# Layer 0's output projection: buffers over other memory, loads in another order, one store on another queue, one context turn later

## The chip, the cores and the metric

The kernel runs on one core of a Trainium2 chip. A core has TensorE (PE: matrix products; PEld is its weight load), VectorE (DVE), ScalarE (ACT) and GpSimd (POOL) for elementwise work, and SyncE (SP), whose queue issues most of the transfers; ScalarE has a queue for transfers too. Every engine works through its own instructions in order and waits on semaphores for the others. The metric is the time of one launch on the device in microseconds (us).

## The reference

Two layers of a diffusion transformer over 1024 latent and 256 context tokens of width 1024, in fp32. Layer 0 is multi-head latent attention (16 heads), layer 1 differential attention (8 heads). What the change touches is the end of layer 0, which for every token is

```python
o = attention(...)                       # (tokens, 1024)
o = o * silu(gate)                       # gated()
x = layer_norm(ALPHA * x + g * (o @ out_w[0]), ln_g[0], ln_b[0])
ctx = layer_norm(ALPHA * ctx + g_c * (o_c @ out_w[0]), ln_g[0], ln_b[0])
```

where `g` and `g_c` are rows of 1024 numbers (the adaptive gates of the latent and of the context tokens), and `x` and `ctx` are what layer 0 was given. The rows so normalised are modulated and become layer 1's input.

## The kernel before

The tokens are ten tiles of 128: tiles 0 to 7 are latent, 8 and 9 context. Products in fp32 are made of three matmuls on operands split into a high and a low part (`mm3`, L184 to L187). A split of an operand is a cast on ScalarE and a subtraction on VectorE (`split`, L176 and L177).

**Layer 0's attention** works head by head. A unit of it is two key tiles: scores on TensorE into a pair of PSUM banks (`pair`), the exponential on ScalarE into a buffer `p32`, a cast to half precision, the remainder on GpSimd (`softmax_parts`, L713 to L715), and later the values on TensorE (L781 to L784); `retire` and `flush` do the values of units that are still pending. The block's end (`fin`, L792 and L793) divides on VectorE into `op`, and at the last head every block stores its part of `op` into the DRAM tensor `o_d[0]` (L797, SP's queue). For the last head the order of the query blocks is 0, 2, 1: the context rows come before the latent rows 512 to 1023.

**The context tiles.** During the last block the two context tiles are loaded from `o_d[0]` with their gates from `sg_d[0]` and multiplied on VectorE (`load_ctx`, L863, L864). `turn_out` transposes a tile on TensorE by eight matmuls with the identity (L834) into two PSUM banks and splits it into the operands of the projection. Tile 8's operands lie in the two buffers `ows`, tile 9's in `rr` and one of the two buffers `cs`. Then `mm_out` makes the projection, a half of the 1024 columns at a time: 8 steps of 3 matmuls of 128x512. The four half products of the context stand in two pairs of banks, `yctx`. TensorE's order is written by hand (`manual_schedule`, MAN = 'P'): turn tile 8, the values of the one unit, turn tile 9, half product of tile 8, `flush` (the values of the last unit), three more half products.

**The output stage** (`with ow_ctx, spool("o0") as op0`) has its own pool of buffers, allocated by `ot`. Its loads are issued from SP: `load_gate` (a gate row to all partitions), `load_res` (what the layer was given), `load_o` (`o` and its gate `g`, multiplied on GpSimd at L993). For every tile `turns` transposes and splits (into `tH`, `tL`), `z_half` multiplies half a product by the gate row, adds the residual and takes statistics (L1004 to L1006), `z_norm` normalises (L1010 to L1012, with two small steps on GpSimd, L159 and L160), `z_keep` writes what layer 1's end needs, and `z_turn` transposes the normalised rows, modulates them on ScalarE and splits them into layer 1's input `h1H`, `h1L` (L1023 to L1029). TensorE's order is by hand here too: turn of tile 0, `z_turn(8)`, half product of tile 0, `z_turn(9)`, turn of tile 1, second half product, and so on.

**Memory.** A pool lays its buffers out in the order in which its tags are first asked for, and a buffer waits for the readers of whatever lay there before (`reuse_waits="tile"`). The pool `o0` lies over the end of the attention's pool. That one has, from the place where `o0` begins, and in kB per partition (1 kB = 1024 B): the end of `op` (1.9), small ones, `rsw` (4), `rr` (4), `stkH`, `stkL`, `stqH`, `stqL`, `stpH`, `stpL` (2.5 each), `ows` (2 x 4), `cs` (2 x 4), `KH0`, `KL0` (2.5 each), `p32` (3 x 4). The buffers of `o0` have 4 kB each (`res`, `o`, `z`, `tH`, `tL` twice, the others once). Before, their order is `gate01` (context gate row, later the norm's gain), `res`, `o`, `g`, `gate00` (latent gate row), `z`, small ones, `tH`, `tL`, `hb`, `gb1`. So `gate01` lies over `op` and `rsw`, the first `res` over `rsw` and `rr`, `o` and `g` over the `st` buffers, and `z` over `ows` and a `cs`.

**The order of the other engines' work**, SP's queue among them, is written by a planner, which starts from the program's order and its own forecast of times. A transfer is issued when SP comes to it and its buffer is free; what is behind it on SP waits with it. PSUM has eight banks; the stage's banks `c`, `b`, `d`, `a` take the place of the attention's three pairs and its two banks `d`.

Of the kernel before, what the change touches and what calls it, by code (L numbers as in the profile page):

```python
# [9 lines left out]
F32 = mybir.dt.float32  # L10
F32R = mybir.dt.float32r
# [6 lines left out]
P = 128  # L18
D = 1024
KT = D // P  # L20
# [8 lines left out]
H0, NOPE, ROPE, V0 = 16, 64, 32, 64  # L29
# [24 lines left out]
def hybrid_kernel(  # L54
# [7 lines left out]
    pe, act, dve, pool, sp = nc.tensor, nc.scalar, nc.vector, nc.gpsimd, nc.sync  # L62
# [6 lines left out]
    def nm(s):  # L69
        uid[0] += 1  # L70
        return f"{s}_{uid[0]}"
# [650 lines left out]
    def retire(part):  # L722

        u = pend[0]
        u[0](*u[1], part)
        if part:
            pend.pop(0)
            if u[2] is not None:
                u[2]()

    def flush():
        while pend:
            retire(0)
            retire(1)
# [20 lines left out]
    def units0(h, b):  # L755
# [30 lines left out]
        def fin():  # L786
            pv = hold["pv"]
            if h % 2 == 0 and b == 0:
                opair[0] = w0("op")
            op = opair[0]  # L790
            rc = w0("rc")
            dve.reciprocal(rc[:, :nt], pv[:, :nt, V0])  # L792
            dve.tensor_tensor(op[:, c0 // P:c0 // P + nt, (h % 2) * V0:(h % 2) * V0 + V0], pv[:, :nt, :V0],  # L793
                              rc[:, :nt].rearrange("p (t o) -> p t o", o=1).to_broadcast([P, nt, V0]), op=ALU.mult)
            if h % 2 == 1 and (b == 2 or h == H0 - 1):
                t0, t1 = (c0 // P, c0 // P + nt) if h == H0 - 1 else (0, NT)
                sp.dma_start(o_d[0].rearrange("(t p) d -> p t d", p=P)[:, t0:t1, (h // 2) * P:(h // 2 + 1) * P],  # L797
                             op[:, t0:t1, :])

        return [((lambda kc=kc: st_of(kc)), do_pv, fin if kc == kcs[-1] else None) for kc in kcs]  # L800
# [38 lines left out]
    def mm_out(y, tH, tL, c):  # L839
        for k in range(KT):  # L840
            mm3(y, tH[:, k, :], tL[:, k, :], oH[:, k, c], oL[:, k, c], k == 0, k == KT - 1)

    yctx = {}
    for h in range(H0):
# [8 lines left out]
        if last:  # L853
# [14 lines left out]
            tv = lambda x: x.bitcast(F32R).rearrange("p (a b) -> p a b", a=KT)  # L868
            tctx = {8: (tv(w0("ows")), tv(w0("ows"))), 9: (tv(w0("rr")), tv(w0("cs")))}
            with tc.manual_schedule(engines={ENG[c] for c in MAN}):  # L870
                for t in (8, 9):
                    tb = pair()
                    turn_out(octx[t][0], *tctx[t], [tb[:, :512], tb[:, 512:]])
                    if t == 8:
                        retire(0)
                        retire(1)
                for t in (8, 9):
                    yctx[t] = pair()
                    for hh in range(2):
                        c = slice(hh * 512, hh * 512 + 512)  # L880
                        mm_out(yctx[t][:, c], *tctx[t], c)
                        flush()
        else:
            kq = chain(prod_k(h + 1), prod_q(h + 1, 0))
# [88 lines left out]
        dve.tensor_tensor(vic, kci, lcf[:, 1:2], op=ALU.mult)  # L973

    with ow_ctx, spool("o0") as op0:
        ot = lambda tag, bufs=2, shape=[P, D], dt=F32: op0.tile(shape, dt, tag=tag, bufs=bufs, name=nm(tag))
        rows_of = lambda t: slice(t * P, (t + 1) * P)
        halves = [slice(hh * 512, hh * 512 + 512) for hh in range(2)]
        gate, gb, res, ol, zs, bs_, tHL = [None] * 2, [], {}, {}, {}, {}, {}
# [1 line left out]
        def load_gate(s):  # L981
            gate[s] = ot(f"gate0{s}", 1)
            bcast_row(gate[s], gates_d[0, s:s + 1, :])
# [5 lines left out]
        def load_o(t):  # L989
            ol[t], g = ot("o"), ot("g", 1)  # L990
            sp.dma_start(ol[t], o_d[0][rows_of(t), :])
            sp.dma_start(g, sg_d[0][rows_of(t), :])
            pool.tensor_tensor(ol[t], ol[t], g, op=ALU.mult)  # L993
# [37 lines left out]
        load_gate(1)  # L1031
        load_res(8)
        load_o(0)
        load_gate(0)
        load_res(9)
        load_o(1)
        for t in (8, 9):
            for hh in range(2):
                z_half(t, hh, yctx[t][:, halves[hh]])
            z_norm(t)  # L1040
# [528 lines left out]
```

## Time and profile before

| | |
|---|---|
| time, median of 3 runs | 1848.2 us (1843.51 to 1848.47) |
| the profiled execution | 1848.19 us |
| its span (first to last instruction) | 1846.4 us |
| mean granted TensorE clock | 0.972 |
| PE busy | 1693.7 us (92%) |
| DVE busy | 1240.0 us (67%) |
| ACT busy | 1104.3 us (60%) |
| POOL busy | 811.8 us (44%) |

The stage in question runs from about 790 to 970 us of the span. How the views are read: a row of the time line has the start, the duration, the engine, the line, the operation, what it writes and reads, a count, and in brackets how long the engine stood idle before it and for whom. A row of the waits has who waited for whom, the sum, how often, and the longest. A row of the table by stretches has the stretch, its length, the busy time and count of PE, PEld, DVE, ACT and POOL, the granted clock, the share of the DMA engines and the GB/s. `SPq` is SP's queue.

### The profile page before, as it was taken

The numbers are of one execution on the slowest core, as the hardware profiler recorded it, in microseconds if no ns is written. First come the engines' busy times: TensorE is split into PE (matmuls) and PEld (weight loads), VectorE is DVE, ScalarE is ACT, GpSimd is POOL, SyncE is SP. The second block draws the span as 40 slices with busy tenths as digits, with TensorE's granted clock in tenths as the row PEclk, the third lists the DMA queues.
The fourth block names the chain that finished last, engine by engine and source line by source line (L and its number), as shares of the span: only waits on it lengthen the run. The fifth ranks groups of instructions, "written<-read, shape, count | busy, mean of one in ns | idle before, by whom it ended". The sixth has DMA issues, their size and how long they took to land. (4 is left out here: it accounts for less than half of the span.)

```text
span 1846.4 us, 36569 instructions
## 1 busy us (share of the span) xinstructions
PE 1693.7 (92%) x14468; PEld 1239.2 (67%) x14468; DVE 1240.0 (67%) x2054; ACT 1104.3 (60%) x2223; POOL 811.8 (44%) x719
## 2 busy tenths in 40 slices
PE   8889999999999999888999999999999999986998
PEld 3889975666666665566776676757575767665776
DVE  6545765565565566627764878777777777879574
ACT  3433047777877778824444675767676776757442
POOL 1434026766867766827542313131313132435454
PEclk8999899999999999999999999999999999999999
DMA  8245631101111121236433212121212122223231
GB/s 290 82 117 170 195 109 35 45 21 44 40 38 32 41 56 48 73 114 211 148 126 84 76 52 73 51 73 51 68 40 58 49 55 62 64 63 109 92 130 69
DMA packets 111225, 154.84 MB, mean 84 GB/s; under 512 B 13415, under 2 KB 84679, under 8 KB 111054
## 3 DMA queue, kind: packets, MB, share of 16 engines
q1 hardware_dynamic: 103182, 145.17, 26.3%
q10 hardware_dynamic: 7872, 7.34, 1.2%
q8 instruction: 114, 1.87, 0.4%
q14 instruction: 57, 0.47, 0.1%
HBM read 98.65 MB, written 27.07 MB: 68 GB/s over the span
## 5 line engine op out<-in xcount | busy, mean ns | idle before, releaser
L715 POOL TENSOR_TENSOR pl<-p,ph 128x1024 f16<-128x1024 f32 (+1 forms) x176 | 364.6, 2077 | 148.9 <-ACT ph L714 122.6
L1251 ACT ACTIVATE p<-ps_b,mx 128x512 f32<-128x512 f32 (+1 forms) x384 | 230.3, 617 | 86.0 <-DVE mx L1247 81.9
L713 ACT ACTIVATE p<-ps_a,esc 128x1024 f32<-128x1024 f32 (+1 forms) x176 | 189.0, 1074 | 96.1 <-PE ps_a L771 89.7
L695 DVE TENSOR_REDUCE mx<-ps_a 128x1 f32<-128x1024 f32 x128 | 155.5, 1223 | 134.8 <-PE ps_a L693 134.7
L714 ACT CAST ph<-p 128x1024 f16<-128x1024 f32 (+1 forms) x176 | 177.1, 1006 | 5.5
L1245 DVE TENSOR_REDUCE mx<-ps_b 128x1 f32<-128x512 f32 x256 | 165.9, 683 | 0.0
L784 PE MATMUL ps_d<-Vh,pl 128*128 128x65 f16 x1344 | 145.9, 194 | 4.7 <-POOL pl L715 4.6
L781 PE MATMUL ps_d<-Vh,ph 128*128 128x65 f16 x1344 | 148.1, 195 | 0.0
L783 PE MATMUL ps_d<-Vl,ph 128*128 128x64 f16 x1344 | 146.9, 193 | 0.0
L1228 PE MATMUL ps_b<-KS,QS 128*128 128x512 f16 (+1 forms) x384 | 126.8, 347 | 12.6 <-DVE pl L182 6.9
L1276 POOL TENSOR_TENSOR sm<-sm,us 128x1 f32<-128x1 f32 x64 | 17.0, 265 | 272.8 <-DVE sm L1255 269.3
L781 PEld LDWEIGHTS <-ph 128*128 128x128 f16 x1344 | 123.2, 97 | 18.3 <-issue 5.1
L783 PEld LDWEIGHTS <-ph 128*128 128x128 f16 x1344 | 123.9, 98 | 12.0
L1229 PE MATMUL ps_b<-KS,Q 128*128 128x512 f16 (+1 forms) x384 | 129.5, 346 | 0.0
L769 PE MATMUL ps_a<-qH,KH 100*128 100x512 f16 x320 | 122.5, 383 | 7.5 <-ACT p L713 3.7
L182 DVE SCALAR_TENSOR_TENSOR pl<-ps_b,lcf,ph 128x512 f16<-128x512 f32 (+1 forms) x192 | 117.3, 655 | 15.0 <-ACT ph L181 14.9
L784 PEld LDWEIGHTS <-pl 128*128 128x128 f16 x1344 | 123.1, 97 | 6.1 <-POOL pl L715 6.1
L181 ACT ACTIVATE ph<-ps_b,lcf 128x512 f16<-128x512 f32 (+1 forms) x192 | 115.0, 646 | 19.7 <-PE ps_b L1264 19.7
L1264 PE MATMUL ps_b<-idr,p 128*128 128x128 f32 x640 | 103.6, 278 | 24.5 <-ACT p L1251 16.3
L770 PE MATMUL ps_a<-qH,KL 96*128 96x512 f16 x320 | 122.3, 382 | 0.0
L771 PE MATMUL ps_a<-qL,KH 96*128 96x512 f16 x320 | 121.7, 380 | 0.0
L1274 PE MATMUL ps_b<-vh,pl 128*128 128x128 f16 x640 | 111.3, 220 | 5.3 <-DVE pl L182 5.3
(412 smaller groups left out, 5294.3 us busy)
## 6 DMA issues: line engine op xcount, KB each, us to landing
ws<-in_dw SPq DMA_DIRECT2D x28, 512.0 KB, 3.9
adw<-in_ada_w SPq DMA_DIRECT2D x24, 512.0 KB, 4.7
adaw<-in_ada_w SPq DMA_DIRECT2D x16, 512.0 KB, 5.9
g<-sg_d SPq DMA_DIRECT2D x16, 512.0 KB, 3.5
sg_d<-gg ACTq DMA_DIRECT2D x40, 128.0 KB, 3.8
o_d<-op SPq DMA_DIRECT2D x7, 640.0 KB, 3.7
xt<-in_xT SPq DMA_DIRECT2D x16, 256.0 KB, 3.2
wgs<-in_w_in SPq DMA_DIRECT2D x32, 128.0 KB, 2.2
```

Source lines behind the costliest of these rows:

```text
L695: dve.tensor_reduce(mx[:, t, 0:1], ps, axis=AX.X, op=ALU.max)
L713: act.activation(p32[:, :n], st, AF.Exp, scale=esc0)
L714: act.copy(ph[:, :n], p32[:, :n])
L715: pool.tensor_tensor(pl[:, :n], p32[:, :n], ph[:, :n], op=ALU.subtract)
L769: pe.matmul(s_, kh[:nr, ks], QH[:nr, :], start=True, stop=False)
L781: pe.matmul(pv[:, t, :], ph[:, ts], Vh[:, k, h, :], start=(k == kcs[0] and t == 0), stop=False, skip_group_check=True)
L783: pe.matmul(pv[:, t, :V0], ph[:, ts], Vl[:, k, h, :], start=False, stop=False, skip_group_check=True)
L784: pe.matmul(pv[:, t, :], pl[:, ts], Vh[:, k, h, :], start=False, stop=(k == NT - 1), skip_group_check=True)
L1228: pe.matmul(out, qs[m][:, ts], ks[m][:, c0:c0 + n], start=True, stop=False)
L1229: pe.matmul(out, q1[m][:, ts], ks[m][:, c0:c0 + n], start=False, stop=True)
L1245: dve.tensor_reduce(mx[:, 2 + 2 * m + i:3 + 2 * m + i], b, axis=AX.X, op=ALU.max, negate=True)
L1251: act.activation(p[m][:, c0:c0 + n], b, AF.Exp, bias=nb, accum_out=sm[:, 2 + 3 * m + i:3 + 3 * m + i])
```

## The change

It has four parts. (1) `ot` allocates by `rot`, and the first buffer of each tag is allocated ahead of the stage in a written order: `gb1`, `gate00`, `hb`, `o`, `g`, `z`, `tH`, `tL`, `gate01`, `res`. So `gb1` lies over `op` and `rsw`, `gate00` over `rsw` and `rr`, `hb` over `rr` and `stkH`; `o` and `g` lie where they lay; `z` lies over `stpL` and `ows`, `tH` over `ows` and `cs`, `tL` over `cs`, `KH0`, `KL0` and a `p32`, `gate01` and `res` over `p32` and behind it. (2) The load of the latent gate row comes after `load_res(9)` and `load_o(1)`. (3) The last store of `op` (last head, block 1) is issued from ScalarE's queue. (4) The turn of tile 9 comes after the first half product of tile 8, ahead of `flush`.

```diff
             if h % 2 == 1 and (b == 2 or h == H0 - 1):
                 t0, t1 = (c0 // P, c0 // P + nt) if h == H0 - 1 else (0, NT)
-                sp.dma_start(o_d[0].rearrange("(t p) d -> p t d", p=P)[:, t0:t1, (h // 2) * P:(h // 2 + 1) * P],
+                (act if h == H0 - 1 and b == 1 else sp).dma_start(
+                    o_d[0].rearrange("(t p) d -> p t d", p=P)[:, t0:t1, (h // 2) * P:(h // 2 + 1) * P],
                              op[:, t0:t1, :])
...
-                for t in (8, 9):
+                def turn_ctx(t):
                     tb = pair()
                     turn_out(octx[t][0], *tctx[t], [tb[:, :512], tb[:, 512:]])
-                    if t == 8:
-                        retire(0)
-                        retire(1)
+
+                turn_ctx(8)
+                retire(0)
+                retire(1)
                 for t in (8, 9):
                     yctx[t] = pair()
                     for hh in range(2):
                         c = slice(hh * 512, hh * 512 + 512)
                         mm_out(yctx[t][:, c], *tctx[t], c)
+                        if t == 8 and hh == 0:
+                            turn_ctx(9)
                         flush()
...
     with ow_ctx, spool("o0") as op0:
-        ot = lambda tag, bufs=2, shape=[P, D], dt=F32: op0.tile(shape, dt, tag=tag, bufs=bufs, name=nm(tag))
+        ot = lambda tag, bufs=2, shape=[P, D], dt=F32, **kw: rot(op0, shape, dt, tag, bufs, **kw)
+        for tag, bufs in (("gb1", 1), ("gate00", 1), ("hb", 1), ("o", 2), ("g", 1), ("z", 2), ("tH", 2), ("tL", 2),
+                          ("gate01", 1), ("res", 2)):
+            ot(tag, bufs, [P, KT, P] if tag in ("hb", "tH", "tL") else [P, D], F32R if tag in ("tH", "tL") else F32,
+               first=True)
...
         load_gate(1)
         load_res(8)
         load_o(0)
-        load_gate(0)
         load_res(9)
         load_o(1)
+        load_gate(0)
```

## The prediction

> **What bounds the kernel now.** I read the page first, then the waits of the stretch around the changed code, then the time line of each engine and the SP queue there, and last a table by stretches. Durations are us from the start of the span. "Tile 8" and "tile 9" are the two context tiles, "tile 0" the first latent one.
>
> ```profile
> span 1846.4 us, 36569 instructions
> ```
>
> The profiled execution took 1848.19 us; the median of the runs is 1848.2, so a sum made against this trace stands for the median as it is. TensorE bounds the kernel as a whole, so what counts is where it stands still. In the waits of all engines from 785 to 850 two of its waits stand out, and one of POOL:
>
> ```profile
> POOL o L993 <- DVE bs L1006: 33.3, 1, 33.3
> ...
> PE ps_c L834 <- POOL o L993: 8.6, 1, 8.6
> ...
> PE ps_a L834 <- DVE cs L864: 2.4, 1, 2.4
> ```
>
> TensorE waits 8.6 us for POOL's gated product of tile 0 (L993) and 2.4 us for VectorE's gated product of tile 9 (L864). POOL did not wait for the statistics of L1006, which have nothing to do with its operands, but for the two loads of L993. Why these came late is told by the waits of the SP queue from 790 to 828, and its time line:
>
> ```profile
> SPq L797 <- DVE op L793: 17.9, 1, 17.9
> SPq L987 <- PE ps_a L186: 9.4, 1, 9.4
> SPq L897 <- DMA o_d<-op: 5.8, 1, 5.8
> ```
>
> ```profile
> 810.99 0.37 SPq L797 DMA_DIRECT2D o_d<-op  x1
> 817.25 0.32 SPq L897 DMA_DIRECT2D gate<-gates_d  x1
> 827.01 0.33 SPq L987 DMA_DIRECT2D res<-in_ctxr  x1
> 827.39 0.42 SPq L991 DMA_DIRECT2D o<-o_d  x1
> 827.91 0.38 SPq L992 DMA_DIRECT2D g<-sg_d  x1
> ...
> 829.30 0.49 SPq L991 DMA_DIRECT2D o<-o_d  x1
> ```
>
> SP works in order. It stood 17.9 us at the last store of the attention output, 5.8 until that store had landed (the context gate row's buffer lies over `op`), and 9.4 until TensorE had read `rr` for the last time (the buffer of `res` lies over `rsw` and `rr`). `o` and `g` of tile 0, whose own memory was long free, were behind. The price on TensorE, by stretches (length, busy time and count of each engine, granted clock, DMA share, GB/s), and its time line with one row of each step:
>
> ```profile
> 798.90:801.30 2.40, 0.02 (x1) 0.00 (x0) 2.40 (x2) 0.30 (x1) 1.21 (x1) 0.98 0.00 0
> 801.30:804.70 3.40, 3.37 (x12) 3.08 (x13) 1.18 (x2) 0.63 (x2) 0.00 (x0) 0.51 0.00 0
> 804.70:827.20 22.50, 22.46 (x117) 17.76 (x115) 2.59 (x5) 0.54 (x1) 0.00 (x0) 1.00 0.33 106
> 827.20:835.80 8.60, 0.03 (x1) 0.03 (x1) 3.89 (x7) 0.00 (x0) 2.34 (x1) 0.77 0.91 320
> 835.80:839.00 3.20, 3.20 (x17) 3.00 (x17) 2.27 (x4) 1.47 (x3) 0.75 (x2) 0.54 0.95 301
> ```
>
> ```profile
> 796.18 1.06 PE L834 MATMUL ps_a<-idr,rsw 128*128 128x128 f32 x8 [0.65 <-DVE rsw L864]
> ...
> 798.73 0.20 PE L784 MATMUL ps_d<-Vh,pl 128*128 128x65 f16 x1
> 801.33 1.94 PE L834 MATMUL ps_a<-idr,cs 128*128 128x128 f32 x8 [2.41 <-DVE cs L864]
> 802.93 0.78 PE L185 MATMUL ps_a<-oH,ows 128*128 128x512 f32 x1
> ...
> 809.38 0.21 PE L781 MATMUL ps_d<-Vh,ph 128*128 128x65 f16 x1
> ...
> 810.12 0.48 PE L185 MATMUL ps_a<-oH,ows 128*128 128x512 f32 x1
> ...
> 826.77 0.40 PE L187 MATMUL ps_a<-oH,cs 128*128 128x512 f32 x1
> 835.77 1.97 PE L834 MATMUL ps_c<-idr,o 128*128 128x128 f32 x8 [8.61 <-POOL o L993]
> ...
> 838.96 0.47 PE L185 MATMUL ps_a<-oH,tH 128*128 128x512 f32 x1
> ...
> 845.61 1.06 PE L1023 MATMUL ps_d<-idr,z 128*128 128x128 f32 x8 [0.80 <-DVE z L1012]
> ```
>
> Behind both standstills the granted clock is about half for some 3.3 us (0.51 and 0.54), and eight transposes take 1.94 and 1.97 us there against 1.06 at full clock. Three half products (24 matmuls each) run from 810.12 to 827.0, 5.64 us each; the values of the last unit take 0.74 (809.38 to 810.12). The rest of the case is what the other engines do:
>
> ```profile
> 795.06 5.04 POOL L715 TENSOR_TENSOR pl<-p,ph 128x1024 f16<-128x1024 f32 x2 [0.44 <-ACT ph L714]
> ```
> ```profile
> 797.89 0.69 DVE L177 TENSOR_TENSOR ows<-ps_a,ows 128x512 fp32r<-128x512 f32 x1 [1.86 <-ACT ows L176]
> 798.50 2.69 DVE L864 TENSOR_TENSOR cs<-cs,cs 128x1024 f32<-128x1024 f32 x1
> 801.11 0.68 DVE L177 TENSOR_TENSOR ows<-ps_a,ows 128x512 fp32r<-128x512 f32 x1
> ```
> ```profile
> 833.38 2.34 POOL L993 TENSOR_TENSOR o<-o,g 128x1024 f32<-128x1024 f32 x1 [33.27 <-DVE bs L1006]
> ...
> 836.93 0.58 ACT L176 CAST tH<-ps_c 128x512 fp32r<-128x512 f32 x1 [31.69 <-PE ps_c L834]
> ...
> 837.54 0.69 DVE L177 TENSOR_TENSOR tL<-ps_c,tH 128x512 fp32r<-128x512 f32 x1
> ```
>
> **Part 1: the turn of tile 9 half a product later.** Before, TensorE goes from the values (798.93) over the wait and the slow transposes to the first product matmul at 802.93. After, the first half product of tile 8 starts at 798.93: its first operands are split by 798.58 (797.89 + 0.69). Its later operands are ready at 801.79 (801.11 + 0.68) and wanted by the 15th matmul, at 798.93 + 14 x 0.235 = 802.22, so 0.4 us hides them. Tile 9's product is ready at 801.19, long before its transposes at 804.6. Their split needs about 3 us on ScalarE and VectorE and has the values (0.74) and a half product (5.64) over it, so it costs nothing; without that cover it would cost about 3. With no standstill I take the clock as full. The context products then end at 798.93 + 4 x 5.64 + 1.06 + 0.74, and 0.16 that the last matmul outlasts the pace: 823.45, against 827.17. **Gain 3.7.**
>
> The clock weighs here: half speed from 801.30 to 804.70 costs half of 3.4 us, 1.7. The Trainium skill, TensorE: Matmul & The Clock Gate, Part 1 (the HAM clock gate), has the clock halved after an idle window of about 3.4 us that runs freely; a standstill of 2.41 us cannot fill one. By that rule the slow stretch would have another cause and could stay: a gain of 2.0 in place of 3.7. The trace has it begin right behind the standstill, and I go by the trace.
>
> **Part 2: the buffers.** With the tags laid out in the new order, the context gate row and `res` lie over the exponentials `p32`, whose last reader is POOL's L715, done at 800.10; `o` and `g` stay where they were. So gate row, `res` and `o`, `g` of tile 0 can be issued from 800.1. Four transfers of 0.52 MB at the 320 GB/s of the stretch 827.20:835.80 take 6.6 us; first data come some 2 us behind the issue (827.39 to 833.38 is 6.0 us for three). They land by about 809, POOL's product is ready by 811.5, 12 us ahead of 823.45. Should the load of `o` have to await the landing of the last store (issued near 807, and 6 us on its way before), the product would end near 821.5: still in time. What is late next: `z` lies over `ows`, free when tile 8's product ends near 812; the gate multiplication, residual sum and norm of tile 8 take about 8 us (6.7 from 830.76 to 836.68 + 0.81 and 1.3 for the multiplication) and end near 820:
>
> ```profile
> 830.76 1.29 DVE L1005 SCALAR_TENSOR_TENSOR z<-res,z 128x512 f32<-128x512 f32 x2 [2.87 <-DMA res<-in_ctxr]
> ...
> 836.68 0.81 DVE L1012 TENSOR_SCALAR z<-z,mv 128x1024 f32<-128x1024 f32 x1 [2.72 <-POOL mv L160]
> ```
> Before, tile 9's `z` lay over an operand of the second context product; now its first half runs beside that product's second half. The two `yctx` pairs and the new banks share PSUM: tile 0's transposes go where tile 8's product lay, and need its gate multiplication done, some 10 us earlier. So nothing holds TensorE at 823.45: eight transposes of tile 0 and eight of tile 8 take 2 x 1.06; the cast and the first subtraction end 2.46 us after the transposes start (835.77 to 837.54 + 0.69), the third matmul wants them at 2.59. I take 2.2 from the end of the context products to the first matmul of tile 0; it was 11.8 (827.17 to 838.96). **Gain 9.6.**
>
> **Part 3: the order of the loads.** The latent gate row moves behind `res` and `o`, `g` of tile 9, and so on SP behind the wait of the second `g` (one buffer) for POOL's first product, which ends by 811.5. It lies over `rr`, so SP then stands until the end of the context products, and behind it stand the lambda row, the first latent `res`, both norm rows and the next loads. Gate row, lambda and `res`, 1.2 MB, land about 5.7 us after 823.45; the multiplication that wants them follows the first half product at 2.2 + 5.64 = 7.8. Hidden by 2 us; were it not, the norm of tile 0 would slip by what is missing. The lambda row stands in VectorE's order ahead of tile 9's norm, which tile 9's transposes await. It was 6.65 us from the first matmul to these (838.96 to 845.61), 0.80 of it the wait; it can be 5.64 and no wait, or with the lambda row landing late a wait of 1.5. I take 0.5. **Gain 0.5 (from -0.5 to 1.0).**
>
> **Part 4: the last store on ScalarE.** 0.37 us of issue, behind a wait until about 807 for VectorE. Behind it ScalarE has three weight loads that wait for the same values anyhow, and the casts of tile 0 at 824.6. Were it still on SP, the loads would go at 807 in place of 800 and the product would be ready near 818.5: still in time. Zero.
>
> Sum: 3.7 + 9.6 + 0.5 = 13.8, so 1848.2 - 13.8 = **1834.4 us**.
>
> What follows has its own waits (the two stretches, and a row of the waits from 845 to 970):
>
> ```profile
> 839.00:970.00 131.00, 123.42 (x600) 96.50 (x599) 94.66 (x126) 57.51 (x123) 76.06 (x52) 0.97 0.45 150
> 970.00:1840.00 870.00, 804.88 (x6432) 593.46 (x6429) 642.98 (x1234) 548.27 (x1479) 284.59 (x398) 0.98 0.24 69
> ```
> ```profile
> PE ps_d L1023 <- DVE z L1012: 6.8, 4, 3.3
> ```
>
> TensorE is idle for 7.6 of the 131 us of the tile loop. The loop's order of loads and of POOL's work shifts against TensorE, so these may change by some 4 us either way: the likeliest case's own range is 1830 to 1839.
>
> **The rivals.** (a) *The loop takes it back.* POOL is busy for 76.06 of the 131 us, and its norm steps queue behind its products; if the loop is paced by it, an earlier start ends in longer waits of the transposes for the norm. Against it: TensorE is busy for 94%, and POOL's first two products move out of the loop's start. One or two more waits like the longest, 3.3 us, take 3 to 7: about 1840. (b) *The queue is held all the same*, by a wait that I do not see, on the first load or by another order of SP that the planner writes. Then only part 1 is left: 1844.5. For it: the waits of one queue hide behind each other, as three did here. (c) *The clock by the rule of the window*: 1.7 us stay, 1836.1. (d) *Slower: the planner's order in layer 1.* Only TensorE's order is written by hand; the planner orders the others by its own forecast, which shifts. Layer 1 has 64 steps in 870 us. A worse order there that costs 0.22 us a step eats all 13.8, and 0.35 makes 1857. Against it: all of layer 1 shifts alike, and its buffers lie where they lay. (e) *The change doesn't do what it says*, no load starts earlier and the turn costs what it saves: 1848.
>
> **How the numbers follow.** Likeliest 0.70, (a) 0.10, (b) 0.06, (c) 0.05, (d) 0.05, (e) 0.04. A measurement of this kernel tells about 0.3%, 5.5 us, from no change: faster is under 1842.7. The likeliest, (a) and (c) are faster: 0.85; (b) and (e) count as the same: 0.10; slower 0.05. The range of 8 in 10 takes in (a) and the loop's spread: 1829 to 1842.
>
> **What would show it.** Right: SP issues six loads between 800 and 803; POOL's L993 runs near 810; no wait of L834 for L993; L185 of tile 8 ahead of tile 9's transposes, which take 1.06; granted clock 1.00 from 799 to 835; tile 0's first matmul near 825.6, tile 9's `z` transposes near 832. Wrong: a wait of SP in front of the six loads, a wait of L1023 over 2 us for the norm, or longer mean times from step to step in layer 1.

## The result, and the profile after

The changed kernel takes **1836.7 us** in the median (1831.31 to 1843.42), the kernel before 1844.3 us beside it: a ratio of **0.9962, interval 0.9945 to 0.9979**. A second set of runs gave 0.9969 (0.9954 to 0.9984). So 6 to 7 us are gained by these ratios (the medians differ by 7.6 and 6.7), half of the 13.8 predicted. The profiled execution of the changed kernel took 1831.31 us, its span is 1829.5 us.

One span less the other (16.9 us) says little: the first attention product (L693) stands at 273.15 and 269.16 us in two profiles of the kernel before, and at 263.87 and 269.75 in two of the changed one, long ahead of anything that was changed. So the stage is measured from an anchor close to it: the last attention product ahead of tile 8's turn that waits for GpSimd (L784). TensorE's time line of the changed kernel, one row of each step (columns as before):

```profile
779.55 0.20 PE L784 MATMUL ps_d<-Vh,pl 128*128 128x65 f16 x1 [0.83 <-POOL pl L715]
787.47 1.06 PE L835 MATMUL ps_a<-idr,rsw 128*128 128x128 f32 x8 [2.89 <-DVE rsw L865]
...
795.18 1.03 PE L835 MATMUL ps_a<-idr,cs 128*128 128x128 f32 x8
...
813.67 1.03 PE L835 MATMUL ps_c<-idr,o 128*128 128x128 f32 x8
821.59 1.94 PE L1031 MATMUL ps_d<-idr,z 128*128 128x128 f32 x8 [6.89 <-DVE z L1020]
823.18 0.78 PE L185 MATMUL ps_a<-oH,tH 128*128 128x512 f32 x1
...
830.81 1.03 PE L1031 MATMUL ps_d<-idr,z 128*128 128x128 f32 x8
...
843.78 1.09 PE L1031 MATMUL ps_d<-idr,z 128*128 128x128 f32 x8
...
942.58 1.04 PE L1031 MATMUL ps_b<-idr,z 128*128 128x128 f32 x8
```

The wait of 2.4 us at tile 9's turn and the 8.6 us at tile 0's are gone. In their place TensorE waits 6.89 us one step later, at the turn of z(8), and the eight transposes behind it take 1.94 us. By stretches (columns as before) it is the same picture: full clock to 813.7, then 7.9 us with 1.0 us of work, then half clock:

```profile
797.50:813.70 16.20, 16.20 (x71) 12.91 (x71) 2.56 (x6) 0.59 (x1) 2.40 (x1) 1.00 0.61 210
813.70:821.60 7.90, 1.01 (x10) 0.80 (x8) 6.77 (x9) 1.07 (x2) 3.06 (x3) 0.90 0.65 230
821.60:825.00 3.40, 3.30 (x11) 2.56 (x12) 3.40 (x7) 2.28 (x7) 0.28 (x2) 0.50 0.62 216
```

The loads did what they were to do. SP's queue of the changed kernel (`SPq` rows) and GpSimd's product of tile 0:

```profile
789.34 0.32 SPq L901 DMA_DIRECT2D gate<-gates_d  x1
789.70 0.43 SPq L995 DMA_DIRECT2D res<-in_ctxr  x1
790.24 0.38 SPq L999 DMA_DIRECT2D o<-o_d  x1
790.72 0.36 SPq L1000 DMA_DIRECT2D g<-sg_d  x1
...
813.63 0.32 SPq L901 DMA_DIRECT2D gate<-gates_d  x1
```
```profile
797.58 2.40 POOL L1001 TENSOR_TENSOR o<-o,g 128x1024 f32<-128x1024 f32 x1 [8.26 <-DVE cs L177]
...
817.75 0.19 POOL L159 TENSOR_SCALAR mv<-mv 128x1 f32<-128x1 f32 x1 [17.78 <-DVE mv L1018]
818.03 0.56 POOL L160 TENSOR_TENSOR mv<-mv,neghalf 128x1 f32<-128x1 f32 x1
818.56 2.34 POOL L1001 TENSOR_TENSOR o<-o,g 128x1024 f32<-128x1024 f32 x1
```

The four loads go at 789.3 to 790.7, 23 to 24 us ahead of the context products' end, and tile 0's product is done at 800. What is late stands in VectorE's time line of the changed kernel:

```profile
802.67 1.29 DVE L1012 TENSOR_TENSOR z<-ps_a,gate 128x512 f32<-128x512 f32 x2 [3.76 <-DMA ws<-in_dw]
813.87 0.69 DVE L1012 TENSOR_TENSOR z<-ps_a,gate 128x512 f32<-128x512 f32 x1 [9.91 <-PE ps_a L187]
814.47 1.28 DVE L1013 SCALAR_TENSOR_TENSOR z<-res,z 128x512 f32<-128x512 f32 x2
815.67 1.28 DVE L1014 BATCH_NORM_STATS2 bs<-z 128x6 f32<-128x512 f32 x2
816.87 0.67 DVE L1012 TENSOR_TENSOR z<-ps_a,gate 128x512 f32<-128x512 f32 x1
817.46 0.20 DVE L1018 BATCH_NORM_AGGREGATE mv<-bs 128x2 f32<-128x12 f32 x1
818.62 2.82 DVE L1020 TENSOR_SCALAR z<-z,mv 128x1024 f32<-128x1024 f32 x1 [0.96 <-POOL mv L160]
```

The two gate products of tile 8 (L1012) run at 802.67. The next instruction in VectorE's queue is not tile 8's residual (L1013) but the first gate product of **tile 9**, and that stands 9.91 us until the last matmul into tile 9's pair of banks. All of tile 8's rest, its data long there, runs behind it. In the kernel before the order is the same, at 820.73, 827.20 and 830.76 (the last row is in the prediction); there it cost nothing, since `res` landed only at 830.7. VectorE's two gate products there:

```profile
820.73 1.29 DVE L1004 TENSOR_TENSOR z<-ps_a,gate 128x512 f32<-128x512 f32 x2 [9.76 <-DMA gate<-gates_d]
827.20 0.69 DVE L1004 TENSOR_TENSOR z<-ps_a,gate 128x512 f32<-128x512 f32 x1 [5.18 <-PE ps_a L187]
```

From the turn of z(7) to the end of the span it is 887.2 and 885.6 us in two profiles before, 886.9 and 885.8 in two after (spans 1846.4, 1839.8, 1829.5, 1833.7 less the row of z(7)): layer 1 did not change.

### The profile page after: what moved, and what is told of

It is laid out like the page before. It is cut to its first block, busy times and chain, and to the rows that moved or that the text cites. A ratio compares the mean times of both kernels' runs of the same rounds, so it can differ in the third digit from the quotient of the medians.

```text
span 1829.5 us, 36574 instructions
## 1 busy us (share of the span) xinstructions
PE 1680.2 (92%) x14468; PEld 1229.2 (67%) x14468; DVE 1238.1 (68%) x2054; ACT 1104.9 (60%) x2223; POOL 812.0 (44%) x719
## 5 line engine op out<-in xcount | busy, mean ns | idle before, releaser
L784 PE MATMUL ps_d<-Vh,pl 128*128 128x65 f16 x1344 | 145.9, 194 | 3.9 <-POOL pl L715 3.9
L784 PEld LDWEIGHTS <-pl 128*128 128x128 f16 x1344 | 123.1, 97 | 5.3 <-POOL pl L715 5.3
```

The source lines that it names most:

```text
L784: pe.matmul(pv[:, t, :], pl[:, ts], Vh[:, k, h, :], start=False, stop=(k == NT - 1), skip_group_check=True)
```

## The experiments

Theory T: the order in VectorE's queue makes the 6.9 us and the half clock. Rivals: D, tile 8's data are late; L, the loop over the tiles takes back whatever comes earlier; S, the store on ScalarE's queue costs something. The table gives, for one profile of every kernel, how far behind the anchor (the L784 above) TensorE reaches a step; each number is the start of the step's row less that of the anchor's. "Context end" is the start of tile 0's transposes less the wait named in their row.

| kernel | anchor | context end | first product, tile 0 | turn z(9) | turn z(0) | turn z(7) | ratio to the kernel before |
|---|---|---|---|---|---|---|---|
| before | 790.50 | 36.7 | 48.5 | 55.1 | 68.2 | 168.7 | – |
| before_2 | 787.65 | 35.9 | 47.7 | 54.9 | 68.0 | 166.5 | – |
| changed | 779.55 | 34.1 | 43.6 | 51.3 | 64.2 | 163.0 | 0.9962 (0.9945 to 0.9979) |
| after_2 | 785.30 | 34.1 | 43.6 | 51.2 | 64.2 | 162.6 | 0.9969 (0.9954 to 0.9984) |
| u_turn | 787.56 | 35.7 | 45.2 | 52.2 | 65.2 | 164.4 | 0.999 (0.9975 to 1.0004) |
| u_bufs | 786.97 | 35.4 | 47.4 | 54.6 | 69.0 | 169.8 | 0.999 (0.9976 to 1.0005) |
| u_loads | 785.62 | 36.3 | 43.8 | 51.3 | 64.3 | 165.0 | 0.9977 (0.9965 to 0.999) |
| u_store | 787.10 | 34.1 | 43.6 | 51.2 | 64.2 | 162.6 | 0.9982 (0.9969 to 0.9995) |
| e_order | 788.24 | 34.1 | 42.6 | 49.0 | 63.7 | 161.0 | 0.995 (0.9933 to 0.9967) |
| e_pool | 782.81 | 35.3 | 42.8 | 50.4 | 65.3 | 165.4 | 0.9973 (0.9958 to 0.9989) |
| e_bank | 788.42 | 34.1 | 41.1 | 49.6 | 63.8 | 161.1 | 0.9973 (0.9962 to 0.9985) |
| e_best | 786.20 | 34.1 | 38.6 | 44.3 | 63.8 | 161.7 | 0.997 (0.9957 to 0.9983) |
| e_clear | 784.29 | 32.4 | 34.1 | 41.2 | 59.7 | 158.0 | 0.9952 (0.9934 to 0.997) |
| e_loop | 784.80 | 36.4 | 38.1 | 44.9 | 59.1 | 158.2 | 0.994 (0.9922 to 0.9959) |

**The parts undone one at a time.** First the buffers:

```diff
-        ot = lambda tag, bufs=2, shape=[P, D], dt=F32, **kw: rot(op0, shape, dt, tag, bufs, **kw)
-        for tag, bufs in (("gb1", 1), ("gate00", 1), ("hb", 1), ("o", 2), ("g", 1), ("z", 2), ("tH", 2), ("tL", 2),
-                          ("gate01", 1), ("res", 2)):
...
+        ot = lambda tag, bufs=2, shape=[P, D], dt=F32: op0.tile(shape, dt, tag=tag, bufs=bufs, name=nm(tag))
```

> Edit: the changed kernel with the old order of buffers (the residual's buffers over memory that is still read by the context products). The prediction put 9.6 us on the buffers. Theory T: with VectorE's order as it is the buffers can have been worth only what the changed kernel shows, from the end of the context products to tile 0's first product 9.5 against 11.8 us: 2 to 3 us, ratio to the kernel before 0.997 to 0.998, and the waits on the loads are back. Rival L (the loads were worth 9.6 us and the loop took 7 back): from the end of the context products 18 us or more to tile 0's first product, ratio near 1.000 or over.

The waits are back. SP's queue of this kernel stands again until TensorE has read `rr` for the last time, and tile 0's turn waits 8.50 us:

```profile
809.30 0.32 SPq L901 DMA_DIRECT2D gate<-gates_d  x1
822.19 0.33 SPq L991 DMA_DIRECT2D res<-in_ctxr  x1
822.57 0.42 SPq L995 DMA_DIRECT2D o<-o_d  x1
```
```profile
830.88 1.97 PE L835 MATMUL ps_c<-idr,o 128*128 128x128 f32 x8 [8.50 <-POOL o L997]
```

From the context's end to tile 0's first product it is 12.0 us against 9.5: 2.4 at this place, as T had it, and 18 or more, as L had it, is far off. The stage up to z(7) is 7 us longer, of which 1.3 come from a half clock ahead of the context's end and 3.6 behind the turn of z(9), in the loop; the ratio, 0.999, lies a little above what T gave, with an interval that holds it.

Then the turn of tile 9:

```diff
-                def turn_ctx(t):
+                for t in (8, 9):
                     tb = pair()
                     turn_out(octx[t][0], *tctx[t], [tb[:, :512], tb[:, 512:]])
-
-                turn_ctx(8)
-                retire(0)
-                retire(1)
+                    if t == 8:
+                        retire(0)
+                        retire(1)
...
-                        if t == 8 and hh == 0:
-                            turn_ctx(9)
```

> Edit: the changed kernel with the turn of tile 9 back ahead of the context products. The prediction put 3.7 us on it. By it the 2.4 us wait and the half clock behind it are back: 3.7 to 4.7 us more than the changed kernel, ratio to the kernel before 0.998 to 0.999; VectorE's chain starts at the end of the context products, so that all behind it moves by the same. Rival D (the chain behind hangs on data that land at a fixed time): the context products end later, the first product of tile 0 doesn't, and the ratio stays at 0.996.

It cost 1.6 us in the profile (35.7 against 34.1) and not the 3.7 to 4.7 expected, and all behind moved with it; D is out. The turn of tile 9 waits again, but shorter than in the first profile of the kernel before, and at full clock:

```profile
799.18 1.06 PE L835 MATMUL ps_a<-idr,cs 128*128 128x128 f32 x8 [1.89 <-DVE cs L865]
```

The ratios (0.999 against 0.9962 and 0.9969) differ by 4 to 5 us, with intervals that overlap, so they don't exclude 1.6. Then the two parts that were priced at little, the store and the order of the loads:

```diff
-                (act if h == H0 - 1 and b == 1 else sp).dma_start(
+                sp.dma_start(
```

> Edit: the changed kernel with the last store back on SP's queue. The prediction put 0 on the store. By it the time stays that of the changed kernel, a ratio to the kernel before of 0.996. Rival S (the store on ScalarE's queue is what moved the sum into rsw against GpSimd's work: in the one profile of the kernel before that sum starts 0.26 us ahead of GpSimd's next operation and takes 1.23 us, in five profiles with the store on ScalarE it starts 0.06 to 0.60 us behind it and takes 2.6 to 3.2 us): the sum takes 1.2 us again and TensorE waits 0.65 us before the turn of tile 8, not 2.9; 2 us less than the changed kernel.

S is out: the sum into `rsw` takes 2.47 us and TensorE waits 2.89 here too. The stage is that of the changed kernel to 0.1 us; the times' intervals (0.9969 to 0.9995 against 0.9945 to 0.9984) overlap, and a cost of the store is not shown.

```diff
+        load_gate(0)
         load_res(9)
         load_o(1)
-        load_gate(0)
```

> Edit: the changed kernel with the load of layer 0's gate row for the image tokens back ahead of res(9) and o(1). The prediction put 0.5 us on the order of the loads. Theory T: tile 8's chain waits for the context products, not for these loads, and tile 9's comes behind it, so nothing moves: the time of the changed kernel, ratio 0.996. If the order of loads carried part of the gain, the wait at the turn of z(8) or of z(9) grows by the 1.4 us that one such load takes.

A miss: the wait at the turn of z(8) did not stay and did not grow, it **fell**, from 6.89 to 4.88 us, in spite of the same order on VectorE. With the old order of loads the product of o(1) comes only at 830.20, and the norm of z(8) takes 0.81 us. The turn of z(7) is no earlier: 2.2 us were lost to a half clock ahead of the context's end, and 2 in the loop, at the turn of z(2): there TensorE stood still for 3.33 us and the transposes took 1.97, where in the changed kernel it stood still for 3.37 us and they took 1.09. VectorE's norm and TensorE's turn of z(8) in this kernel:

```profile
826.91 0.81 DVE L1020 TENSOR_SCALAR z<-z,mv 128x1024 f32<-128x1024 f32 x1 [0.96 <-POOL mv L160]
```
```profile
827.87 1.94 PE L1031 MATMUL ps_d<-idr,z 128*128 128x128 f32 x8 [4.88 <-DVE z L1020]
```

**The kernel before, once more,** for the chance in a single profile.

> The kernel before, unchanged, for a second profile. Rival S (above) has TensorE wait 0.65 us before the turn of tile 8 in it, as in its first profile. If the sum into rsw meets GpSimd's operation by the chance of when its load lands, a second profile may have 2.9 us there. From the context products' end to tile 0's first product both have 11.8 us, since that hangs on the loads behind the buffers. The time up to layer 0's attention may differ by some us between the two profiles of one kernel.

The chance it is: the wait ahead of tile 8's turn is 2.89 us in this profile, without any change. TensorE, VectorE and GpSimd of the second profile of the kernel before:

```profile
795.58 1.07 PE L834 MATMUL ps_a<-idr,rsw 128*128 128x128 f32 x8 [2.89 <-DVE rsw L864]
799.27 1.06 PE L834 MATMUL ps_a<-idr,cs 128*128 128x128 f32 x8 [1.89 <-DVE cs L864]
```
```profile
792.61 2.82 DVE L864 TENSOR_TENSOR rsw<-rsw,rr 128x1024 f32<-128x1024 f32 x1 [6.62 <-DMA rsw<-o_d]
```
```profile
792.22 5.20 POOL L715 TENSOR_TENSOR pl<-p,ph 128x1024 f16<-128x1024 f32 x2 [0.44 <-ACT ph L714]
```

When the sum into `rsw` starts 0.26 us ahead of GpSimd's next operation, it takes 1.2 us (the first profile before, and e_clear); when it starts 0.06 to 0.9 us behind (the other twelve), it ends 3.2 us after that operation began. With tile 9's turn late that is worth 1.7 us at the context's end (32.4 in e_clear against 34.1). With the turn in its old place it turned round: in the first profile the second sum then met GpSimd (the 2.69 us of the prediction's rows), the turn waited 2.41 us with half clock in place of 1.89 without, and the context's end came 0.8 us later than in the second.

And the changed kernel once more, beside e_clear:

> The changed kernel once more, unchanged, on the same chip as the run beside it: a second profile of it, and its time. Expected: a ratio of 0.996, the wait of 6.9 us at the turn of z(8) again, and 163 us (162 to 165) from the last attention product that waits for GpSimd to the turn of z(7).

All as expected: 6.89 us again, and 162.6 us.

**The collision on the norm.** Now GpSimd's product of o(1) behind the two `rstd`, VectorE's order as it was (`load_o(1)` gives its product back, to be issued later):

```diff
-        load_o(1)
+        mul1 = load_o(1)
...
+        with tc.manual_schedule(engines={ENG["G"]}):
             for t in (8, 9):
...
                 z_norm(t)
+            mul1()
```

> Edit: the changed kernel, with GpSimd's product of o(1) put behind the two rstd of the context tiles; VectorE's order stays. In the changed kernel the norm of z(8) took 2.82 us beside that product (2.34 us) and 0.81 us elsewhere. Theory P (the two engines stand in each other's way while both run): the norm takes 0.81 us, the wait at the turn of z(8) falls from 6.9 to about 4.9 us, and the kernel is 2 us shorter than the changed one, ratio to the kernel before 0.995. If the long norm has another cause, the norm stays at 2.8 us and the wait at 6.9. Tile 9's norm meets the product instead, and has some 4 us to spare. Theory T alone says nothing on this; of its 6.9 us these 2 would be P's share.

P holds: VectorE's norm of z(8) takes 0.81 us, and TensorE's wait is 4.88.

```profile
823.02 0.81 DVE L1021 TENSOR_SCALAR z<-z,mv 128x1024 f32<-128x1024 f32 x1 [0.96 <-POOL mv L160]
...
827.90 2.87 DVE L1021 TENSOR_SCALAR z<-z,mv 128x1024 f32<-128x1024 f32 x1 [0.40 <-POOL mv L160]
```
```profile
823.98 1.94 PE L1032 MATMUL ps_d<-idr,z 128*128 128x128 f32 x8 [4.88 <-DVE z L1021]
```

Tile 9's norm meets the product instead (the second row). So of the 6.9 us, 2.0 are this collision, and 4.9 are left for the order. The ratio did not follow: at the turn of z(7) this kernel is some 2.5 us behind the changed one, with 1.2 more up to the context's end (the granted clock is 0.78 from 790.7 to 798.5) and a wait of 4.05 us with half clock in the loop. The Trainium skill, SBUF — State Buffer, "SBUF: two separate sides", describes a port pair shared by these two engines as "an exclusive lock, not a bandwidth split". The traces agree: in the changed kernel the product began first (818.56) and ran its usual 2.34 us, and the norm ended 0.5 us behind it.

**VectorE's order.** `z_ctx(t)` is the body of the old loop: the halves and the norm of one tile.

```diff
-        for t in (8, 9):
-            for hh in range(2):
-                z_half(t, hh, yctx[t][:, halves[hh]])
-            z_norm(t)
+        with tc.manual_schedule(engines={ENG["P"], ENG["D"]}):
+            z_ctx(8)
...
+            tb = pair()
+            turn_out(ol[0], *tHL[0], [tb[:, :512], tb[:, 512:]])
+            z_ctx(9)
...
-        turns(0)
```

> Edit: the changed kernel, with VectorE's and TensorE's order written out for the two context tiles: all of tile 8's gate product, residual, statistics and norm; then the turn and the split of tile 0; then tile 9's. Nothing is added or left out. Theory T (in the changed kernel tile 9's first gate product stands in VectorE's queue ahead of tile 8's residual, waits there for the last context product, and holds tile 8's norm behind it): the wait of 6.9 us at the turn of z(8) is gone, the eight transposes take 1.06 us and not 1.94, and from the end of the context products to tile 0's first product it is 2.2 to 3 us, not 9.5; with the half clock behind it gone, 7 to 8 us less than the changed kernel, about 1829 us where that has 1837, a ratio to the kernel before of 0.990 to 0.993. Rival D (tile 8's data are late: residual, gate or o land only by then): nothing changes, ratio 0.996. Rival L (the loop over the tiles takes it back): the wait goes, but the turn of z(7) comes less than 3 us sooner, ratio 0.995.

Half a miss. VectorE did as told, but TensorE waited 5.86 us all the same. The ratio (0.995) and the turn of z(7), 1.6 to 2.0 us sooner, are as L had them, but not by its way: the wait, which would be gone by L, is still there. VectorE's norm of z(8) and its second gate product of tile 9, and TensorE's turn:

```profile
816.75 0.81 DVE L1020 TENSOR_SCALAR z<-z,mv 128x1024 f32<-128x1024 f32 x1 [0.96 <-POOL mv L160]
...
828.52 0.67 DVE L1012 TENSOR_TENSOR z<-ps_a,gate 128x512 f32<-128x512 f32 x1
```
```profile
829.25 1.97 PE L1031 MATMUL ps_d<-idr,z 128*128 128x128 f32 x8 [5.86 <-DVE z L1012]
```

The norm is done at 817.6, 4.8 us ahead of the context's end (822.36), so D is out. But the turn starts when tile 9's gate product ends (829.19). The edit had moved more than the order: with tile 0's transposes in a third pair, the banks of the next stage were laid out anew, so that `d`, into which z(8) is transposed, should lie over yctx[9]. In the changed kernel `d` would lie where tile 9's transposes were, and be free. So this run does not yet test T; the wait it shows is of its own making. The next kernel takes other banks for the turn:

```diff
-        y1 = bank("b")
-        z_turn(8)
+        z_turn(8, "b")
+        y1 = bank("b")
```

> Edit: the kernel of the run with VectorE's order written out, and the turn of z(8) now into the two PSUM banks of tag b in place of d (y1 takes one of b behind it). In that run the norm of z(8) was done 4.8 us before the context products ended and the turn waited 5.86 us all the same, until tile 9's second gate product had read its PSUM tile. Theory B (tag d lies over the banks of yctx[9], and the turn waits for these to be read): the wait goes now, the turn takes 1.06 us, and tile 0's first product starts 2.2 to 3 us behind the context products, not 8.5; against the changed kernel that is 6.5 to 7.3 us at this place. The turn of z(9) comes too early for its norm then and waits some 2 us. In all 6 to 8 us less than the changed kernel up to the loop, a ratio to the kernel before of 0.991 to 0.993. Rival (the wait has another source, or all is given back in the loop): the ratio stays at 0.995.

B holds for the turn, which follows tile 0's at once: with VectorE's order turned and the bank free, the wait of 6.89 us at the turn of z(8) is gone. The ratio, 0.9973, is not in the 0.991 to 0.993 expected. The same wait stands one step further, at tile 0's first product:

```profile
829.56 0.77 PE L185 MATMUL ps_a<-oH,tH 128*128 128x512 f32 x1 [5.12 <-DVE wsq L968]
```

It begins 0.15 us after tile 9's second gate product ends (828.74 + 0.67): in this layout it is y0 that lies over yctx[9], as a run further down bears out. The next kernel keeps the banks, but brings tile 9's gate products forward on VectorE (with the split of tile 0's first half ahead of the statistics) and lambda's operations back:

```diff
+            z_half(9, 0, yctx[9][:, halves[0]], lambda: split0(0))
+            split0(1)
+            z_half(9, 1, yctx[9][:, halves[1]])
+            z_norm(9)
...
-        lambda_of()
+        with tc.manual_schedule(engines={ENG["D"]}):
+            lambda_of()
```

> Edit: as the run with tag b, and VectorE does tile 9's first gate product and residual in the gap before tile 0's first split, and lambda's operations are emitted behind tile 9's norm. Theory: z(9)'s norm ends about 8 us behind the context products and not 11 to 14, so that its turn waits for nothing; 1 to 2 us less than the run with tag b, a ratio to the kernel before of 0.990 to 0.992. If the place is not bound by VectorE any more, the same as that run.

The turn of z(9) comes 7.0 us sooner than in the changed kernel (44.3 against 51.3), and the turn of z(0) 0.5 us sooner: L, nearly in full. The ratio is 0.997, where 0.990 to 0.992 was expected. TensorE, ScalarE and GpSimd of this kernel:

```profile
841.73 0.79 PE L185 MATMUL ps_a<-oH,tH 128*128 128x512 f32 x1 [3.75 <-ACT tH L176]
```
```profile
838.30 2.91 ACT L1036 ACTIVATE hb<-ps_d,ab 128x128 f32<-128x128 f32 x8 [5.51 <-POOL h1L L1039]
841.05 0.63 ACT L176 CAST tH<-ps_c 128x512 fp32r<-128x512 f32 x1
```
```profile
830.62 2.79 POOL L1086 TENSOR_SCALAR gate<-gate 128x1024 f32<-128x1024 f32 x1 [2.95 <-DMA gate<-in_ln_g]
833.38 2.77 POOL L1086 TENSOR_SCALAR gb<-gb 128x1024 f32<-128x1024 f32 x1
836.11 2.15 POOL L1039 TENSOR_TENSOR h1L<-hb,h1H 128x1024 f16<-128x1024 f32 x1
```

GpSimd scales the two norm rows, for the first of which it waits 2.95 us, ahead of `h1L` of z(8); ScalarE's `hb` of z(9) waits for that (one buffer); tile 1's cast stands behind `hb`, and TensorE waits 3.75 us for the cast. The next kernel clears this and y0's bank: the tags `c` and `d` are taken ahead, and GpSimd's order is by hand, first `h1L` of z(8) and then the two scalings.

```diff
-        with tc.manual_schedule(engines={ENG["D"]}):
-            lambda_of()
...
-        z_turn(8, "b")
+        mg = ExitStack()
+        mg.enter_context(tc.manual_schedule(engines={ENG["G"]}))
+        with tc.manual_schedule(engines={ENG[c] for c in "AD"}):
+            z_turn(8, "b")
+            lambda_of()
         y1 = bank("b")
+        bank("c"), bank("d")
...
+                mg.close()
```

> Edit: as the run with tile 9's first operations in VectorE's gap, and two more places freed that stopped it: y0's bank lies apart from the banks of yctx[9] and of tile 0's transposes (two tiles of tags c and d are taken first), and GpSimd makes h1L(8) ahead of the two scalings of gate01 and gb1, with ScalarE's exponential of lambda behind hb(8). In the run before this one tile 0's first product waited 2.56 us for the bank, tile 1's 3.75 us for tH behind hb(9), which waited 5.5 us for h1L(8) behind the scalings, and the turn of z(0) came no sooner than in the changed kernel, counted from the last attention product. Theory T, all of it: the first product of tile 0 starts 2.2 to 2.8 us behind the context products (9.5 in the changed kernel), the turn of z(9) some 9 us behind them (17.2), the turn of z(0) 22 us behind them (30.1); 7 to 8 us less than the changed kernel up to there, and, the rest of the loop being the same, a ratio to the kernel before of 0.991 to 0.993. Rival L (the engines that feed the loop, ScalarE and GpSimd, bound tile 0 and 1 by themselves): the turn of z(0) stays 28 us or more behind the context products and the ratio at 0.996 to 0.997.

Tile 0's first product comes 1.7 us behind the context's end and the turn of z(9) 8.8: T in full to there. The turn of z(0) comes 27.3 us behind it, not 22 and not 30, and the ratio is 0.9952, where T gave 0.991 to 0.993. TensorE's row, and what GpSimd does ahead of tile 0's `rstd` (L159):

```profile
843.97 1.97 PE L1033 MATMUL ps_d<-idr,z 128*128 128x128 f32 x8 [5.31 <-DVE z L1022]
```
```profile
839.80 2.34 POOL L1001 TENSOR_TENSOR o<-o,g 128x1024 f32<-128x1024 f32 x1 [1.13 <-DMA g<-sg_d]
842.22 0.19 POOL L159 TENSOR_SCALAR mv<-mv 128x1 f32<-128x1 f32 x1
```

The statistics are done at 837.65 (837.44 + 0.21); the product of o(3) stands ahead of the `rstd` in GpSimd's queue, and its load is late. The last kernel writes GpSimd's order for the whole loop:

```diff
-                    pool.tensor_scalar(gb[j], gb[j], ALPHA, None, op0=ALU.mult)
-                mg.close()
+                    if j == 0:
+                        pool.tensor_scalar(gb[j], gb[j], ALPHA, None, op0=ALU.mult)
+                load_o(2)
             z_turn(t - 1 if t else 9)
+            if 0 < t < 6:
+                load_o(t + 2)
...
             z_norm(t)
+            if t == 0:
+                pool.tensor_scalar(gb[1], gb[1], ALPHA, None, op0=ALU.mult)
             z_keep(t)
...
-            if t < 6:
-                load_o(t + 2)
+        mg.close()
```

> Edit: as the run with y0's bank set apart, and GpSimd's order in the loop over the tiles written out: h1L of the last tile, the product of o(t+2), the rstd of tile t, the residual's sum; the scaling of gb1 behind the rstd of tile 0. In the run before this one the turn of z(9) came 8.8 us behind the context products (17.1 in the changed kernel), but the turn of z(0) waited 5.31 us: tile 0's statistics were done 4.6 us before GpSimd made their rstd, since the product of o(3) stood ahead of it in GpSimd's queue and waited for its load. Theory T: the rstd follows the statistics at once, the turn of z(0) comes about 22 us behind the context products and not 27.3, the waits of 2 to 3.4 us at the turns of z(1) and z(2) shrink, the half clock behind them goes; the last turn of the loop, z(7), comes 153 to 157 us behind the last attention product that waits for GpSimd (158.0 in the run before, 163.0 and 162.6 in the changed kernel), and the ratio to the kernel before is 0.989 to 0.993. Rival: a next wait of the loop (the loads of o and g with their single buffer, ScalarE, VectorE) takes its place and the ratio stays at 0.995.

The wait at z(0) falls to 1.03 us and the turn comes 22.7 us behind the context's end; to the turn of z(7) it is 158.2 us, 4.6 less than the changed kernel's mean, although this profile lost 2.3 us to a half clock ahead of the context's end. TensorE's turn of z(0):

```profile
843.91 1.09 PE L1033 MATMUL ps_d<-idr,z 128*128 128x128 f32 x8 [1.03 <-DVE z L1022]
```

The later waits of the loop stay (2.25 and 2.42 us at two turns), z(7) misses T's 153 to 157, and the ratio is a little short of what T expected: **0.994 (0.9922 to 0.9959)**, a median of 1832.5 us. The interval holds the rival's 0.995 as well. It is the lowest median of the study, 4 us below the changed kernel's; the intervals of the two overlap, and so do those of e_order and e_clear.

## Why the prediction was half right

**Direction and mechanism of the loads: right.** SP issued the four loads at once when GpSimd had read `p32`, the product of tile 0 was done 14 us ahead of its use, no turn of tile 0 waited for it, and the first half product of tile 8 ran ahead of tile 9's turn at full clock. Of the six loads named as the sign of this, four went; `res` of tile 9 and `o` of tile 1 came 10 and 12 us later (800.71 and 803.06). The product of o(1) then ran right behind the `rstd` and waited for no load.

**Part 2, 9.6 us: the step that failed.** "The gate multiplication, residual sum and norm of tile 8 take about 8 us … and end near 820", and so "nothing holds TensorE at 823.45". The 8 us were counted from the moment the operands are there; VectorE's queue was not read. The rows for it stood in the time line before, where they are shown above: L1004 of tile 9 at 827.20 between tile 8's L1004 at 820.73 and its L1005 at 830.76. Measured from the context's end to tile 0's first product: 11.8 before, 9.5 after, a gain of 2.3. The sign that the prediction gave for being wrong, a wait of this turn of over 2 us for the norm, is what came, with 6.89. Of these 6.9 us 2.0 are the norm's collision with GpSimd's product (e_pool), the other 4.9 the order. With VectorE's order turned, the norm off the collision and y0 in banks of its own (e_clear), the context's end is followed by tile 0's first product 1.7 us later: the 2.2 of the prediction were to be had, but not with this order.

**Part 1, 3.7 us: right in kind, mis-sized.** Counted from the anchor, the sum has the context's end at 32.95 us (823.45 - 790.50). e_clear, where the sum into `rsw` starts ahead of GpSimd's operation as in the profile that was read, has 32.4; the changed kernel's two profiles, where it starts behind, have 34.1. So the step holds for the row it was read from, but only 2 of the 14 profiles have that row. The two profiles of the kernel before stand 2.5 and 1.8 us behind the changed ones at the context's end, and undoing this part costs 1.6 in the profile. The half clock that the sum counted as 1.7 is in one profile out of two of the kernel before. Rival (c), that the half clock behind 2.41 us has another cause and stays, is not what came: the changed kernel has a clock of 1.00 from 787.4 to 813.7. But it was right to doubt that a standstill of this length always brings it.

**Part 3, 0.5 us:** at its place it was a loss of 2.0. With the loads in the new order the product of o(1) is ready just when the norm of z(8) runs (wait 6.89 against 4.88 in u_loads). The 6.65 us from tile 0's first product to the turn of z(9) became 7.6 (823.18 to 830.81) and not 5.64, since the half clock lies in it. u_loads lost its lead again at z(2), where one execution has a half clock and the other not, so a gain of the new order in the loop is not shown.

**Part 4, zero:** right within what was measured.

**The loop and the other rivals.** From the turn of z(9) to that of z(7) it is 113.6 and 111.7 us before, 111.8 and 111.4 after: the loop took nothing back, the spread of 4 us given for it held. What rival (a) has in mind does exist: in e_best all but 0.5 of 7.0 us were taken back at the first turn of the loop, by ScalarE and GpSimd. In the changed kernel too little came early for it to show. Rivals (b), (d) and (e) are out by the SP rows, by the equal time of layer 1, and by the result. By the steps, at z(7), the changed kernel is 3.5 to 6.1 us ahead of the two profiles before; the times say 6 to 7.

**The time itself, in part by luck.** 1836.7 us lies 2.3 from the 1834.4 forecast, with half the gain, because the 1848.2 that the sum started from, a median of three runs, was 3.9 above the 1844.3 of all seven runs beside the changed kernel. From 1844.3 the same 13.8 would have given 1830.5.

What stays open: how much of the difference between the ratios of u_turn and u_store and that of the changed kernel is scatter of the runs (the intervals are 0.13 to 0.17% either way); the single profiles show 1.6 and 0 us.

## What to carry to other kernels

When a wait is to be removed, list every semaphore on which the waiting instruction and those behind it hang: the engine's queue ahead of the producer, the memory under the destination, the other engines beside it. An instruction in a queue that cost nothing beside a late load becomes the bound when the load is no longer late, and an edit that sets it right can move banks and queues elsewhere, which its run then measures too. Before a stall from one profile goes into a sum, ask whether a second execution has it: a race of 0.3 us moved 1.7 us here.

## What the runs showed that I had not expected

- **A standstill of 2 to 3.5 us is followed by half clock in some executions and not in others.** Behind 2.41 us (before) the transposes took 1.94, behind 2.89 they took 1.06 in the changed kernel and 1.94 in e_loop and u_loads, behind 3.26 us 1.97 (before) and behind 3.37 and 3.45 us 1.09 and 1.10 (changed kernel, its second profile); behind every one of 4.05 us or more 1.94 to 1.97. The transposes alone don't tell all: in e_pool and u_bufs they took 1.07 and 1.06 behind 2.9 us, and the half clock came right after them (granted clock 0.78 from 790.7 to 798.5, 0.81 from 794.8 to 803.8). The Trainium skill, TensorE: Matmul & The Clock Gate, Part 1, calls the activity window free-running and the number of cold matmuls at a kernel's start run-variable. The traces agree that it varies from one execution to the next, but not with the reading taken in the prediction, that a standstill shorter than some 3.4 us cannot do it.
- **The front of the kernel scatters by 9 us** between executions, in code that the change does not touch (first L693 at 263.9 to 273.2 us in the 14 profiles, with a mean granted clock of 0.95 and 0.91 over the first 300 us at these two ends). A gain of 7 us is smaller than that, so stages have to be compared from an anchor close to them.
- **In this kernel a wait for a PSUM pair is for all of it.** The first half of tile 9's product was done 5.6 us ahead of the second, in a bank of its own, and its gate product still waited for the last matmul of the pair (9.91 us in the changed kernel). In e_best, where VectorE's order puts the first half first by hand, it is the same: 4.99 us, to 820.52, 0.2 us behind the context's end.
